# Element-wise work of w_up's operands on Pool beside VectorE: one decoder layer on one core

## The chip, the cores and the metric

The kernel runs on one core of one Trainium2 chip. The metric is the device time of one execution in microseconds (us), lower is better. The engines of the core are TensorE (PE in the profile, its weight loads PEld), VectorE (DVE), ScalarE (ACT), Pool (POOL, also GpSimd) and SyncE (SP), which here only queues transfers (DMAs).

## What is computed

One layer of a decoder, for 512 tokens of a prompt and 8 samples of 8 new tokens, 576 tokens in all (NT = 576, HALF = 288), with a width of 2048 and a feed-forward width of 5632. A mixer (gated delta heads and mLSTM heads) comes first; then the part that this case is about, the convolutional feed-forward block:

```
h = _rmsnorm(x, norm_ffn_g)
u = jnp.einsum('bld,df->blf', h, w_up)
uc, ffn_new = _causal_dwconv(u, ffn_buf, ffn_conv_w)
uc = uc + ffn_conv_b.astype(f32)
gate, up = jnp.split(uc, 2, axis=-1)
x = x + jnp.einsum('blf,fd->bld', (jax.nn.silu(gate) * up).astype(x.dtype), w_down)
```

The width of `u` is 2 x 5632 = 88 tiles of 128 columns: 44 gate tiles and 44 up tiles. A final norm ends the layer.

## The kernel before, in words

**Numbers in two parts.** Each float32 operand of a large product is split (`split`, lines 118 to 121) into a high part, which ScalarE rounds (L120), and a low part, the difference, which VectorE computes (L121). Each product is then three: high by high, high by low and low by high. In the profile `wh` and `wl` are the parts of weights, `bh` and `bl` those of the right operands in the sevenfold form below, `ah` and `al` those of the activations in the plain form.

**Order.** TensorE's instructions stay in the order in which the program writes them. Those of the other engines are ordered by a scheduler when the program is built, by priorities and a cost model; `urgent` and `ahead` raise a priority. On the chip each engine then runs its own list strictly in that order, and each instruction waits for the semaphores it needs. Work that runs beside the products is written as generators: `spawn` adds one, and `tick` (called once for each 128 rows of a product) moves each of them one step on.

**The plain tiles of w_up.** The first three gate tiles and up tiles (NPL = 3) are plain products of 2048 rows (L198). The last of the three pairs is made by turns (`dense_pair`, line 220), so that the first rows of the activations are done with early. VectorE multiplies each result by the norm's factors into a buffer with pads for the convolution (L1130; the pads and the saved states are small Pool copies, L1074, L1075 and L1080). `conv_rest` (line 1078) convolves on ScalarE (L1083) and VectorE (L1085). `hidden` (line 1092) takes silu of the gate on ScalarE (L1094) and multiplies it by up on VectorE, 512 columns for the prompt (L1096) and 64 for the samples (L1097); `later` (line 183) then queues the store of the result on SyncE (L187), six ticks on.

**The seven products.** The other 41 pairs of tiles use seven products of half size in place of eight (`pair`, line 1274, products at L1265). They need sums and differences of the weights (VectorE, L1230) and, once for all pairs, of the normalised input: the right operands. `prep` (line 1164) makes these for each k of 0 to 7. It loads rows k and k + 8 of x (L1178, into `y`, two buffers for each of the two rows), multiplies them by the norm's factors (VectorE, L1179), and calls `right_operands` (line 1185), which forms four differences of 288 columns (L1188) in the tiles `y1`, `y2` and `t` (one buffer) and splits seven half-width operands in four steps, one of them half as wide. For k = 0 to 4 this runs as a generator beside the plain tiles. For k = 5 to 7 it runs in `seven_start` (line 1145), with a raised priority, as memory comes free: there the pools `b2` (their operands) and `ur` (weights) take over the memory of the plain form's activations.

The first pair's products 0, 4 and 5 are begun over k = 0 to 4 and then completed over k = 5 to 7 (in `pair`). The weights' loads (L129 plain, L1206 sevenfold), the loads of rows of x and the stores of hidden rows share SyncE's queue.

**Later.** w_down has blocks of plain and of seven products; `down_prep` (line 1414) calls the same `right_operands` for the latter. `pair` calls the same `hidden`.

Of the kernel before, what the change touches and what calls it, by code (L numbers as in the profile page):

```python
# [8 lines left out]
F32 = mybir.dt.float32  # L9
F32R = mybir.dt.float32r  # L10
AF = mybir.ActivationFunctionType
ALU = mybir.AluOpType

P = 128
D = 2048
KT = 16
SEQ = 512
NB = 8
# [9 lines left out]
KS = 6  # L28
# [15 lines left out]
# columns of the parameter array  # L44
G1, G2, G3, CW, DG, MG, FW, FBI, GB, AL, M0, NPAR = 0, 16, 32, 48, 144, 145, 153, 417, 505, 506, 507, 515
# columns of the constant array
C_ID, C_INC, C_LV, C_IS, C_BM, C_SG, C_BD, C_RB, C_M3, NCON = 0, 128, 256, 640, 704, 712, 713, 841, 849, 853

# order of the 128-column tiles of w_in
# [19 lines left out]
class Layer:  # L69
# [25 lines left out]
    def open(self, name, **k):  # L95
        """A pool that close() ends (last in, first out on its side of the memory)."""
        stack = ExitStack()
        self.stacks[name] = stack
        return stack.enter_context(self.tc.tile_pool(name=name, **k))
# [57 lines left out]
    def down_weights(self, b):  # L157
        """The weights of the plain blocks from b on, up to the next one of seven products."""
        while b < len(BLOCKS) and BLOCKS[b][1] == FB:
            for mp in range(8):  # L160
                yield self.I["w_down"][sum(n == FB for _, n in BLOCKS[:b]), mp], b == len(BLOCKS) - 1
            b += 1

# [19 lines left out]
    def later(self, n, out, in_):  # L183
        """A store, queued n steps from now."""
        def gen():
            yield n
            self.nc.sync.dma_start(out=out, in_=in_)  # L187
        self.spawn(gen(), prio=False)
# [12 lines left out]
    def dense(self, outs=None):  # L201
        """One 128-column tile of a K=2048 product."""
        pd = None
        if outs is None:
            pd = self.psd()
            outs = (pd[:, 0, 0:HALF], pd[:, 1, 0:HALF])
        for u in range(2):
            for i, part in enumerate(self.unit()):
                self.dense_part(outs, part, 2 * u + i)
        return pd  # L210
# [9 lines left out]
    def dense_pair(self):  # L220
        """Two tiles by turns, so that the first rows of the input are done with early."""
        pds = [self.psd(), self.psd()]
        for u in range(2):
            for pd in pds:
                for i, part in enumerate(self.unit()):
                    self.dense_part((pd[:, 0, 0:HALF], pd[:, 1, 0:HALF]), part, 2 * u + i)
        return pds
# [22 lines left out]
    def sum_bc(self, ss):  # L250
        """Sums over partitions of ss [P, NT], on all partitions."""
        pss = []
        for hf in range(2):
            pr = self.psr()
            sl = slice(hf * HALF, (hf + 1) * HALF)
            self.nc.tensor.matmul(pr[:, 0:HALF], self.ones, ss[:, sl], start=True, stop=True)  # L256
            pss.append((pr[:, 0:HALF], sl))
        return pss
# [139 lines left out]
    def gate_rows(self, outs):  # L398
# [19 lines left out]
        # softplus(y) = max(y, 0) + log1p(exp(-|y|)), log1p(e) = 2 atanh(e / (2 + e))  # L418
# [40 lines left out]
        # gated delta rows: log decay G, -exp(G), exp(Glast - G)  # L459
# [6 lines left out]
        # mLSTM rows (partitions 64-67)  # L466
# [51 lines left out]
    def conv_in(self, t, pd):  # L518
        """Depthwise convolution and silu of a projected tile."""
# [27 lines left out]
    def decay(self, bc, cols):  # L547
        """exp(min(bc_i - col_j, 0)) on and above the diagonal, else 0 (rows j, columns i)."""
        nc = self.nc
        V, A, Pl = nc.vector, nc.scalar, nc.gpsimd  # L550
        em = self.r()
        for c in range(NCH):
            sl = slice(c * CH, c * CH + CH)
            V.tensor_scalar(out=em[:, sl], in0=bc[:, sl], scalar1=cols[c][0], scalar2=0.0, op0=cols[c][1], op1=ALU.min)
        V.tensor_scalar(out=em[0:64, SEQ:NT], in0=bc[0:64, SEQ:NT], scalar1=cols[4][0], scalar2=0.0, op0=cols[4][1], op1=ALU.min)
        A.activation(em[:, 0:SEQ], em[:, 0:SEQ], AF.Exp)
        A.activation(em[0:64, SEQ:NT], em[0:64, SEQ:NT], AF.Exp)
        ev = em[:, 0:SEQ].rearrange("p (c i) -> p c i", c=NCH)
        Pl.tensor_tensor(out=ev, in0=ev, in1=self.bc4(self.con[:, C_INC:C_INC + P]), op=ALU.mult)
        Pl.tensor_tensor(out=em[0:64, SEQ:NT], in0=em[0:64, SEQ:NT], in1=self.con[0:64, C_IS:C_IS + 64], op=ALU.mult)  # L560
        return em
# [7 lines left out]
    def lasts_of(self, bc):  # L569
        """The columns of bc at each chunk's last token."""  # L570
        t = self.sm(12, "last")
        A = self.nc.scalar
        A.copy(t[:, 0:4], bc[:, 0:SEQ].rearrange("p (c i) -> p c i", c=NCH)[:, :, CH - 1])
        A.copy(t[:, 4:12], bc[:, SEQ:NT].rearrange("p (b i) -> p b i", b=NB)[:, :, LS - 1])
        return t

    def dn_head(self, h, q, k, v, sz):
# [14 lines left out]
        # natural k, norms of k  # L592
# [30 lines left out]
        # U = c_j (k_j . k_i) E, KQ = (k_j . q_i) E  # L623
# [19 lines left out]
        # v / |k| natural  # L643
# [18 lines left out]
        # chunk by chunk over the prompt  # L662
# [32 lines left out]
        # output norm; the scale of q only enters through the guard  # L695
# [10 lines left out]
    def pack(self, t, n, tag, order):  # L706
        """32 rows of t at a time as three groups of rows, each the high or the low parts."""
# [11 lines left out]
    def masked_rows(self, vp, g, b, nb):  # L719
        """The rows of vp for nb samples from b on, side by side, with zeros for the other samples' tokens."""  # L720
# [46 lines left out]
    def inverse(self, U, res, more):  # L767
        """X = (I + U)^-1 for the strictly upper part of U: the diagonal blocks of SB by substitution, block by
        block on the partitions, then by doubling."""
# [58 lines left out]
        # blocks of 32 from those of 16  # L828
# [19 lines left out]
        # blocks of 64 from those of 32  # L848
# [19 lines left out]
        # the whole blocks  # L868
# [200 lines left out]
    def conv_pads(self, f):  # L1069
        """A buffer for the depthwise convolution: [2 zeros, prompt, 8 x (2 old, 8 new tokens)]."""  # L1070
        rb = self.rw()
        pads = rb[:, 514:594].rearrange("p (b w) -> p b w", b=NB)
        with self.urgent():
            self.nc.gpsimd.memset(rb[:, 0:2], 0.0)  # L1074
            self.nc.gpsimd.tensor_copy(pads[:, :, 0:2], f[:, 1:9])  # L1075
        return rb, (rb[:, 2:2 + HALF], rb[:, 2 + HALF:514], pads[:, :, 2:10])
# [11 lines left out]
    def psum_parts(self, p0, p1):  # L1088
        """The three parts of conv_pads' buffer in two products by halves of the tokens."""
        return (p0, p1[:, 0:SEQ - HALF], p1[:, SEQ - HALF:HALF].rearrange("p (b w) -> p b w", b=NB))  # L1090

    def hidden(self, j, g, u, o):
# [3 lines left out]
        nc.vector.tensor_tensor(out=o[:, 0:SEQ], in0=g[:, 0:SEQ], in1=u[:, 0:SEQ], op=ALU.mult)  # L1096
        nc.vector.tensor_tensor(out=o[:, SEQ:NT].rearrange("p (b w) -> p b w", b=NB), in0=sv(g), in1=sv(u), op=ALU.mult)  # L1097
        self.later(6, self.hid[j], o[:, 0:NT])

    def ffn(self):  # L1100
# [6 lines left out]
        for j in range(NPL):  # L1107
# [24 lines left out]
            self.hidden(j, hs[0][0], hs[1][0], hs[0][1])  # L1132
# [12 lines left out]
    def seven_start(self):  # L1145
        """After the last plain products: the other right operands and the first left ones."""
# [17 lines left out]
    def prep(self, k0, k1, pool):  # L1164
        """The right operands of the seven half-size products, in two parts, of the rows k and k + 8 of the
        normalised input B: [B11, T3, B21, B22, T1, T2, T4]."""
# [7 lines left out]
        for k in range(k0, k1):  # L1174
# [7 lines left out]
            self.right_operands(*both[k - k0], *y, self.stg.tile([P, NT], F32, tag="t", name=self.nm("t")))  # L1182
            yield YP

    def right_operands(self, hi, lo, y1, y2, t):
        V = self.nc.vector
        A0, A1 = slice(0, HALF), slice(HALF, NT)
        sub = lambda o, a, b: V.tensor_tensor(out=o, in0=a, in1=b, op=ALU.subtract)  # L1188
# [11 lines left out]
    def operands(self):  # L1200
        """The left operands of the seven products of each pair of tiles of w_up, in the order of their use."""
# [72 lines left out]
    def pair(self, j, fst, steps):  # L1274
        """A gate tile and its up tile by seven products of half the size (Winograd's form of Strassen's)."""
# [52 lines left out]
        self.hidden(j, g, u, rg)  # L1328
# [85 lines left out]
    def down_prep(self, f0):  # L1414
        """The right operands of the seven products for the hidden rows f0 + k and f0 + KS + k."""
        self.bh, self.bl = [], []
        both = [[self.sx.tile([P, 7 * HALF], F32R, tag=f"b{n}{k}", name=self.nm("b" + n)) for n in "hl"] for k in range(KS)]
        for k in range(KS):
            y1, y2 = (self.load_hidden(self.r(), f0 + k + KS * i) for i in range(2))
            self.right_operands(*both[k], y1, y2, self.r())  # L1420
            yield

    def down_operands(self, ns):
        """The left operands of the seven products of each pair of tiles of w_down, in the order of their use."""
# [52 lines left out]
    def down_last(self, acts):  # L1477
        """The last block by tokens, so that the final norm of one part runs beside the other part's products."""
# [163 lines left out]
```

## Time and profile before

| | us |
|---|---|
| three runs, median (lowest to highest) | 2703.66 (2702.69 to 2705.25) |
| span of the profiled execution | 2704.9 |
| busy: TensorE / VectorE / ScalarE / Pool | 2661.1 / 1992.4 / 1072.4 / 327.8 |
| the last plain product of w_up ends | 1236.15 |

The page gives the span of the profiled execution, from its first instruction to its last; no other time is listed for that execution. It lies inside the three runs.

How to read the views: a row of the list of waits names the engine that waited, its tile and line, what it waited for, and then the total, the number of waits and the longest, in us. A row of the timeline gives start, length, engine, line, operation, output and inputs with their shapes, a count if several were merged, and in brackets the idle time before it with its releaser. A row for one line gives the shortest, median and longest duration in ns, then the first and the last start in us. `x1024` is a number of columns for each of 128 partitions. Successive VectorE instructions overlap by a little in these records.

### The profile page before, as it was taken

How to read it: one execution, taken by the hardware profiler on the slowest of the kernel's cores; microseconds unless marked ns; L12 is line 12 of the kernel's file. 1: busy time of each engine (PE TensorE's matmuls, PEld its weight loads, DVE VectorE, ACT ScalarE, POOL GpSimd, SP SyncE). 2: the span in 40 equal slices, each digit the busy share in tenths (PEclk: the TensorE clock that was granted, in tenths of full speed). 3: DMA queues.
4: the chain of work that ended last, by engine and by line, in shares of the span. 5: the costliest groups of instructions: out<-in, count | busy, mean ns of one | idle time of the engine just before them, and what ended most of it. 6: DMA issues, size and time to landing. Idle time of an engine off the chain costs nothing.

```text
span 2704.9 us, 48701 instructions
## 1 busy us (share of the span) xinstructions
PE 2661.1 (98%) x19895; PEld 2620.4 (97%) x19895; DVE 1992.4 (74%) x3346; ACT 1072.4 (40%) x1694; POOL 327.8 (12%) x637
## 2 busy tenths in 40 slices
PE   7999999999999999998999999999999999999998
PEld 7999999999999999998999999999999999999998
DVE  7887777764444332289888888888888888988656
ACT  5334344433333232254444444444444443434324
POOL 2223222222111001111000000000000100000001
PEclk9999999999999999999999999999999999999999
DMA  5222222223332334444333333333333373342333
GB/s 195 85 79 92 91 83 91 91 88 105 112 107 89 122 127 134 137 124 149 107 107 107 109 111 110 107 107 107 107 107 107 107 255 99 105 145 71 121 96 100
DMA packets 112233, 304.02 MB, mean 112 GB/s; under 512 B 21912, under 2 KB 28184, under 8 KB 112008
## 3 DMA queue, kind: packets, MB, share of 16 engines
q1 hardware_dynamic: 107896, 291.17, 34.1%
q0 software_dynamic: 1872, 7.37, 0.8%
q8 instruction: 156, 2.56, 0.4%
q10 hardware_dynamic: 2240, 2.36, 0.3%
q14 instruction: 69, 0.57, 0.1%
HBM read 264.79 MB, written 36.06 MB: 111 GB/s over the span
## 4 chain that ended last, share of the span: by engine, by line
PE 88%; DVE 4%; DMA 1%; ACT 1%; issue 1%; POOL 0%; SPq 0%; DVEq 0%
PE pd L198 35%; PE pr L1265 31%; PE pd L1265 12%; PE pr L198 3%; PE pr L1491 1%; DMA r<-hid 1%; PE pr L991 1%; DVE wl L121 1%; PE pr L737 1%; DVE bl L121 0%; POOL irk L613 0%; DVE r L1526 0%; PE pr L832 0%; PE pr L256 0%; ACT r L603 0%
## 5 line engine op out<-in xcount | busy, mean ns | idle before, releaser
L120 ACT CAST wh<-raw 128x1024 fp32r<-128x1024 f32 (+1 forms) x394 | 404.6, 1027 | 744.7 <-PE pd L198 410.6
L1265 PE MATMUL pr<-bh,wh 128*128 128x288 f32 x2120 | 627.5, 296 | 2.2 <-ACT bh L120 2.2
L1265 PE MATMUL pr<-bl,wh 128*128 128x288 f32 x2120 | 625.0, 295 | 0.7 <-DVE bl L121 0.6
L1265 PE MATMUL pr<-bh,wl 128*128 128x288 f32 x2120 | 625.2, 295 | 0.1
L121 DVE TENSOR_TENSOR wl<-raw,wh 128x1024 fp32r<-128x1024 f32 (+1 forms) x394 | 474.4, 1204 | 183.3 <-ACT wh L120 177.0
L198 PE MATMUL pd<-ah,wh 128*128 128x288 f32 x2496 | 558.4, 305 | 0.0
L198 PE MATMUL pd<-ah,wl 128*128 128x288 f32 x2496 | 534.4, 296 | 0.0
L198 PE MATMUL pd<-al,wh 128*128 128x288 f32 x2496 | 534.2, 296 | 0.0
L198 PEld LDWEIGHTS pd<-ah,wh 128*128 128x128 f32 x2496 | 401.0, 189 | 9.5 <-issue 2.9
L198 PEld LDWEIGHTS pd<-ah,wl 128*128 128x128 f32 x2496 | 401.9, 189 | 0.0
L1265 PEld LDWEIGHTS pr<-bl,wh 128*128 128x128 f32 x2120 | 400.7, 189 | 1.1 <-DVE bl L121 1.1
L198 PEld LDWEIGHTS pd<-al,wh 128*128 128x128 f32 x2496 | 401.8, 189 | 0.0
L1265 PEld LDWEIGHTS pr<-bh,wh 128*128 128x128 f32 x2120 | 399.3, 188 | 2.4 <-ACT bh L120 2.4
L1265 PEld LDWEIGHTS pr<-bh,wl 128*128 128x128 f32 x2120 | 399.5, 188 | 0.8 <-DVE wl L121 0.8
L120 ACT CAST wh<-s 128x1024 fp32r<-128x1024 f32 (+1 forms) x171 | 169.5, 991 | 362.9 <-DVE s L1230 139.3
L1265 PE MATMUL pd<-bh,wh 128*128 128x288 f32 x848 | 252.0, 297 | 5.6 <-ACT wh L120 5.6
L1265 PE MATMUL pd<-bh,wl 128*128 128x288 f32 x848 | 250.9, 296 | 1.7 <-DVE wl L121 1.7
L1265 PE MATMUL pd<-bl,wh 128*128 128x288 f32 x848 | 249.9, 295 | 0.0
L121 DVE TENSOR_TENSOR wl<-s,wh 128x1024 fp32r<-128x1024 f32 (+1 forms) x171 | 196.5, 1149 | 27.0 <-ACT wh L120 19.6
L1265 PEld LDWEIGHTS pd<-bh,wh 128*128 128x128 f32 x848 | 160.2, 189 | 6.1 <-ACT wh L120 6.1
L1265 PEld LDWEIGHTS pd<-bh,wl 128*128 128x128 f32 x848 | 160.7, 189 | 2.3 <-DVE wl L121 2.3
L1265 PEld LDWEIGHTS pd<-bl,wh 128*128 128x128 f32 x848 | 160.9, 190 | 0.0
(391 smaller groups left out, 3514.1 us busy)
## 6 DMA issues: line engine op xcount, KB each, us to landing
raw<-in_w_up SPq DMA_DIRECT2D x176, 512.0 KB
raw<-in_w_in SPq DMA_DIRECT2D x114, 512.0 KB
raw<-in_w_down SPq DMA_DIRECT2D x40, 512.0 KB
raw<-in_w_out SPq DMA_DIRECT2D x32, 512.0 KB
raw<-in_w_down SPq DMA_DIRECT2D x40, 384.0 KB
hid<-r SPq DMA_DIRECT2D x44, 288.0 KB
r<-hid SPq DMA_DIRECT2D x40, 288.0 KB
r<-in_xT SPq DMA_DIRECT2D x32, 288.0 KB
```

The lines of the kernel that those rows point to most:

```text
L120: nc.scalar.copy(hi, src)
L121: nc.vector.tensor_tensor(out=lo, in0=src, in1=hi.bitcast(F32), op=ALU.subtract)
L198: mm(outs[hf], w, x[:, hf * HALF:(hf + 1) * HALF], start=first and i == 0, stop=last and i == 2)
L737: mm(pr[:, 16 * b:16 * b + 16], st[:, b], kqs[:, b].rearrange("p a w -> p (a w)"), start=True, stop=True)
L991: mm(pn[0:64, 0:257], self.qim[:, b], caug[b // 4][:, b % 4], start=b == 0, stop=False)
L1265: mm(out, w[:, ks], x[:, sl], start=k == 0 and i == 0, stop=k == nk - 1 and i == 2)
L1491: mm(pr[:, 0:n], w[:, ks], acts[kk][:, a * NT + sl.start:a * NT + sl.stop], start=kk == 0 and i == 0, stop=kk == FB - 1 and i == 2)
```

## The change

`hidden` and `right_operands` get the engine as a parameter. The three plain pairs of tiles pass Pool to `hidden`, `pair` passes VectorE as before. `prep` passes Pool to `right_operands`, `down_prep` passes VectorE as before. The splits' differences (L121) stay on VectorE, and so does the multiplication by the norm's factors (L1179). Nothing else differs but comments, which keep their lines as empty ones.

```
-    def hidden(self, j, g, u, o):
+    def hidden(self, j, g, u, o, e):
...
-        nc.vector.tensor_tensor(out=o[:, 0:SEQ], in0=g[:, 0:SEQ], in1=u[:, 0:SEQ], op=ALU.mult)
-        nc.vector.tensor_tensor(out=o[:, SEQ:NT].rearrange("p (b w) -> p b w", b=NB), in0=sv(g), in1=sv(u), op=ALU.mult)
+        e.tensor_tensor(out=o[:, 0:SEQ], in0=g[:, 0:SEQ], in1=u[:, 0:SEQ], op=ALU.mult)
+        e.tensor_tensor(out=o[:, SEQ:NT].rearrange("p (b w) -> p b w", b=NB), in0=sv(g), in1=sv(u), op=ALU.mult)
...
-            self.hidden(j, hs[0][0], hs[1][0], hs[0][1])
+            self.hidden(j, hs[0][0], hs[1][0], hs[0][1], Pl)
...
-            self.right_operands(*both[k - k0], *y, self.stg.tile([P, NT], F32, tag="t", name=self.nm("t")))
+            self.right_operands(*both[k - k0], *y, self.stg.tile([P, NT], F32, tag="t", name=self.nm("t")), nc.gpsimd)
...
-    def right_operands(self, hi, lo, y1, y2, t):
-        V = self.nc.vector
+    def right_operands(self, hi, lo, y1, y2, t, e):
...
-        sub = lambda o, a, b: V.tensor_tensor(out=o, in0=a, in1=b, op=ALU.subtract)
+        sub = lambda o, a, b: e.tensor_tensor(out=o, in0=a, in1=b, op=ALU.subtract)
...
-        self.hidden(j, g, u, rg)
+        self.hidden(j, g, u, rg, V)
...
-            self.right_operands(*both[k], y1, y2, self.r())
+            self.right_operands(*both[k], y1, y2, self.r(), self.nc.vector)
```

## The prediction

> **What bounds the kernel now.** I read the page's busy shares first, then the list of what TensorE waited for, then the stretches around the place that the change touches, and last each engine's order of time there.
>
> ```profile
> PE 2661.1 (98%) x19895; PEld 2620.4 (97%) x19895; DVE 1992.4 (74%) x3346; ACT 1072.4 (40%) x1694; POOL 327.8 (12%) x637
> ...
> PE pd L1265 <- ACT wh L120: 4.0, 1, 4.0
> PE pr L1265 <- ACT bh L120: 2.2, 1, 2.2
> PE pd L1265 <- DVE wl L121: 0.9, 1, 0.9
> PE pr L1265 <- DVE bl L121: 0.6, 1, 0.6
> ```
>
> TensorE (PE) is busy for 98% of the span, so work taken off VectorE (DVE) can only pay where TensorE waits for it. The four lower rows are all the waits of TensorE between 1130 and 1300 us, the stretch that holds every moved instruction: 7.7 us in all. The stretches place them (columns: length, then busy time of PE, PEld, DVE, ACT, POOL, granted clock, DMA):
>
> ```profile
> 1172.00:1229.00 57.00, 57.00 (x429) 57.00 (x428) 54.68 (x95) 27.53 (x39) 5.25 (x12) 1.00 0.47 144
> 1229.00:1236.15 7.15, 7.15 (x56) 7.15 (x55) 4.07 (x7) 4.58 (x7) 1.87 (x3) 1.00 0.04 15
> ...
> 1236.15:1242.15 6.00, 1.97 (x16) 1.74 (x15) 5.61 (x9) 1.44 (x3) 0.00 (x0) 0.91 0.75 234
> 1242.15:1247.23 5.08, 4.13 (x16) 3.79 (x16) 5.08 (x10) 2.08 (x4) 0.54 (x2) 0.50 0.69 252
> ...
> 1250.65:1254.10 3.45, 0.66 (x3) 0.45 (x4) 3.45 (x6) 1.50 (x3) 0.00 (x0) 1.00 0.37 122
> 1254.10:1258.05 3.95, 3.95 (x21) 3.95 (x20) 3.95 (x6) 2.73 (x5) 0.72 (x1) 0.58 0.12 35
> ```
>
> Until 1236.15 the last plain tiles of w_up run and TensorE never stops, although VectorE is nearly full. Then the seven products begin, and TensorE stands twice: 1238 to 1244 and 1250.65 to 1254. After each stand its granted clock is about half for some 4 us (0.50, 0.58). In both VectorE is full. This handover is the one place where the change can move the end.
>
> **The change, part by part.** It moves 32 subtractions of 128x288 (four for each of eight row pairs k) and three pairs of products (128x512 and 128x64) from VectorE to Pool.
>
> ```profile
> L1188 DVE TENSOR_TENSOR t<-y x8: 447/450/456, 1181.9 to 1250.1; 128x288 f32<-128x288 f32 x8
> L1499 POOL TENSOR_TENSOR r<-r,r x12: 732/868/1223, 2649.4 to 2690.5; 128x320 f32<-128x320 f32 x6, 128x256 f32<-128x256 f32 x6
> 1147.91 1.77 POOL L1052 TENSOR_TENSOR r<-r,r 128x576 f32<-128x576 f32 x1 [11.78 <-ACT r L1051]
> L1038 DVE SCALAR_TENSOR_TENSOR al<-r,par,ah x16: 805/805/1830, 1147.6 to 1163.6; 128x576 fp32r<-128x576 f32 x16
> ```
>
> One subtraction takes VectorE 0.45 us, of which 0.08 overlaps its successor (two that follow each other start 0.37 apart, below): 0.37 us come free for each. On Pool the nearest row is L1499: 0.73 us for its 256 columns at the least, 0.87 in the middle, mostly 320; for 288 I take 0.80.
>
> These 0.80 us do not run wholly beside VectorE. The last row shows VectorE's slowest case, 1830 ns in place of 805, and it is the one during which Pool's 576-column addition runs: VectorE was held for 1.03 us. Half the columns hold it for half, 0.53 us (estimate; it could be the whole 0.80). So each moved subtraction frees 0.37 and holds 0.53: VectorE loses 0.16 us a piece where it is full, and its own instruction in progress first delays Pool's. The Trainium skill ("SBUF — State Buffer", Who interferes with whom) says that a VectorE instruction with two SBUF inputs and a Pool one that reads SBUF exclude each other, whichever starts first; the trace agrees with its 1830 ns.
>
> *Plain tiles, to 1236 us: 0.* Twenty subtractions of k = 0 to 4 and three of k = 5 cost VectorE 23 x 0.16 = 3.7 us; the products of tiles 0 and 1 at 512 columns hold 0.94 and free some 0.6, twice, 0.7 more. Against 4.4 us stand idle 57.00 - 54.68 + 7.15 - 4.07 = 5.4 us. The cover is thin, but the operands are first read after 1236, and the weights' splits that TensorE reads here come ahead of need: TensorE waits for none. Without the cover the excess would land on the handover, a few tenths of a us.
>
> ```profile
> L1096 DVE TENSOR_TENSOR r<-r,r x44: 682/691/693, 1196.4 to 2173.5; 128x512 f32<-128x512 f32 x44
> L814 POOL TENSOR_TENSOR r<-r,con x16: 1277/1494/2012, 124.0 to 600.0; 128x512 f32<-128x512 f32 x16
> 1197.20 0.32 SPq L187 DMA_DIRECT2D hid<-r  x1
> 1199.88 0.33 SPq L129 DMA_DIRECT2D raw<-in_w_up  x1
> 1272.59 0.33 SPq L187 DMA_DIRECT2D hid<-r  x1
> 1276.87 3.10 SPq L1206 DMA_DIRECT2D raw<-in_w_up  x2
> ```
>
> *silu(gate) * up: 0.* The product grows from 0.69 to about 1.49 us (0.8 later), the small one, an eighth of the columns, by 0.1 (estimate), and each may wait a VectorE instruction. Its store stands in SyncE's queue ahead of weight loads; those went out 2.7 us (first tile) and 4.3 us (third) after the store, so 1 to 3 us more are covered, nearly. Pool's queue holds behind these only the small copies of the convolution's pads and states, needed a tile later, and the state's DMAs, for which TensorE does not wait.
>
> *Handover.* First VectorE, then ScalarE and SyncE, in order of time:
>
> ```profile
> 1236.17 0.76 DVE L1130 TENSOR_TENSOR r<-pd,rstd 128x288 f32<-128x288 f32 x2 [2.71 <-PE pd L198]
> 1236.85 0.75 DVE L121 TENSOR_TENSOR bl<-y,bh 128x576 fp32r<-128x576 f32 x1
> ...
> 1238.18 1.42 DVE L121 TENSOR_TENSOR bl<-y,bh 128x576 fp32r<-128x576 f32 x2
> 1239.71 1.22 DVE L1230 TENSOR_TENSOR s<-raw,raw 128x1024 f32<-128x1024 f32 x1
> 1240.86 0.45 DVE L1188 TENSOR_TENSOR y<-y,t 128x288 f32<-128x288 f32 x1
> 1241.57 0.82 DVE L1179 SCALAR_TENSOR_TENSOR y<-y,par,rstd 128x576 f32<-128x576 f32 x1 [0.26 <-DMA y<-x2d]
> ...
> 1242.67 1.22 DVE L121 TENSOR_TENSOR wl<-s,wh 128x1024 fp32r<-128x1024 f32 x1
> 1243.81 0.45 DVE L121 TENSOR_TENSOR bl<-y,bh 128x288 fp32r<-128x288 f32 x1
> 1244.17 1.22 DVE L1230 TENSOR_TENSOR s<-s,raw 128x1024 f32<-128x1024 f32 x1
> ...
> 1246.55 1.22 DVE L121 TENSOR_TENSOR wl<-s,wh 128x1024 fp32r<-128x1024 f32 x1
> ...
> 1249.40 0.80 DVE L1179 SCALAR_TENSOR_TENSOR y<-y,par,rstd 128x576 f32<-128x576 f32 x1
> ...
> 1251.63 0.45 DVE L1188 TENSOR_TENSOR y<-y,y 128x288 f32<-128x288 f32 x1
> 1252.00 0.45 DVE L1188 TENSOR_TENSOR t<-y,t 128x288 f32<-128x288 f32 x1
> ```
> ```profile
> 1234.11 0.66 ACT L120 CAST bh<-y 128x576 fp32r<-128x576 f32 x1
> 1236.17 0.33 SPq L1206 DMA_DIRECT2D raw<-in_w_up  x1
> 1237.62 0.33 SPq L1178 DMA_DIRECT2D y<-x2d  x1
> ...
> 1244.29 0.33 SPq L1178 DMA_DIRECT2D y<-x2d  x1
> ```
> ```profile
> 1237.62 3.92 DMA y<-x2d
> ```
>
> The stall of 4.0 us ends with the first sum s of weights (1239.71) and its cast. The sum needs the weights asked for at 1236.17, as the last plain product freed their memory, and a smaller load asked for at 1237.62 took 3.92 us; so VectorE cannot bring the sum much forward: 0, or up to 0.53 later behind one Pool hold.
>
> The stall of 0.9 us ends with the split wl at 1242.67, which the same VectorE queue delivers after a subtraction, the norm and another subtraction. The next sum and split follow (1244.17, 1246.55), just in time for TensorE at 1247.2. I take the freed subtractions here as used up by Pool's holds, and two holds more in this chain: +1.1 us (ends: -0.9, the stall gone, and +2.1, four holds).
>
> The two last stalls, 2.2 + 0.6 us, wait for k = 7. Its second row could be loaded only at 1244.29, when k = 5's last split (1243.81) had let go of the buffer; that split needed the subtraction at 1240.86, which queued on VectorE behind splits and the sum, though its input was split by 1238.9. On Pool it starts then: waiting 0.7 for VectorE's split, 0.8, a cast of 0.4 and a split of 0.4 bring the load to about 1241.9, landing 3.92 later at 1245.8. Norm (0.8, after a wait of 1), a Pool subtraction (0.8 and 0.7 of waiting), cast and split (0.7 each) end near 1250.5, and TensorE, itself 1.1 later, asks for them near 1251.5. So 2.8 us go: -2.8. What is late next is the sum of weights, counted above.
>
> With that stand its slow clock goes too: 3.95 x (1 - 0.58) = 1.7 us. The Trainium skill ("TensorE: Matmul & The Clock Gate", What's actually happening) has the clock fall after an idle window of about 3.4 us; by that, stalls of 2.2 and 0.6 us need not have cost it and I would forecast 1.7 us less gain. The row says 0.58, and the measurement decides.
>
> Sum: 0 + 0 + 1.1 - 2.8 - 1.7 = -3.4 us. The profiled span is 2704.9 us, 1.2 above the median of 2703.66 and inside the three runs (2702.69 to 2705.25); taken off the median it is **2700.3 us**.
>
> **Rivals.** Measurement can tell some 0.2% here, 5.4 us.
>
> *Pool's chain becomes the late one (slower).* Each subtraction of k = 7 on which its casts wait would take 0.80 plus a wait for a VectorE split of up to 1.14, in place of 0.37: three make 4.7 us, and four holds in the weights' chain 2.1 us, while stalls and slow clock stay: +6.8, 2710.5 us. It decides once k = 7's subtractions end after about 1252. For: the 1830 ns, and VectorE full. Against: in the old order these stood behind weights' sums anyway. Chance 0.15.
>
> *No earlier than before.* Each engine's order is fixed when the program is made. If the norm of k = 7's second row keeps its place (1249.40), the subtraction ends at 1250.1 + 0.8 + up to 1.1 = 1252.0, where it ends now: 2703.7 us, give or take 1. Chance 0.18.
>
> *All but the first stall goes.* VectorE sat 2.71 us before 1236.17, its queue standing at L1130, while the cast of 1234.11 had made its next split ready. With fewer instructions the order may put those splits first; then no hold falls into the weights' chain: -2.8 - 0.9 - 1.7 = -5.4, and 1 or 2 more if the clock of 0.50 recovers sooner: 2696.5 to 2698.3 us. Chance 0.25.
>
> **How the numbers follow.** The forecast has 0.42 (its own range 2698.5 to 2703). Faster by over 5.4 us: 0.15 of the third rival and 0.02 of the forecast. Slower: 0.12 of the first. The rest, 0.71, is within 0.2%. The range 2696 to 2709.5 leaves out the ends of the third and the first, some 0.15.
>
> **What would show it.** Right: TensorE waits for bh or bl after 1250 are gone, the stretch after has clock 1.00, the second y load goes out before 1243, subtractions on Pool take 0.8 to 1.9 us, and some VectorE instructions there are 0.5 longer. The forecast is wrong if TensorE waits in the plain tiles, if the sum at 1239.7 starts over 1 us later, or if TensorE's waits change after 1270, where I expect none.

## The result, and the profile after

The change makes the kernel slower by about 17 us, three times the 5.4 us that the prediction held for measurable.

| | before | after |
|---|---|---|
| median of 4 runs each (lowest to highest), us | 2704.1 (2702.69 to 2705.25) | 2722.34 (2719.01 to 2724.08) |
| ratio, 95% interval | | 1.0063 [1.0051, 1.0076] |
| span of the profiled execution, us | 2704.9 | 2722.3 |
| last plain product of w_up ends, us | 1236.15 | 1250.42 |

Of the 17.4 us between the spans, 14.3 lie ahead of the last plain product (1250.42 - 1236.15) and 3.1 behind it. The forecast had put nothing at all into the first part.

Lines of the changed kernel stand one lower behind line 1186: the subtractions are L1187, the weights' sums L1229, the loads L1205, the seven products L1264. First its busy shares:

```profile
PE 2666.9 (98%) x19895; PEld 2624.7 (96%) x19895; DVE 1991.6 (73%) x3308; ACT 1073.2 (39%) x1694; POOL 373.8 (14%) x675
```

The work did move: VectorE has 38 instructions fewer and Pool 38 more, 46.0 us of them. But VectorE's busy time fell by 0.8 us only; what stayed on it grew by nearly as much as was taken off. Then what TensorE waited for from 1130 to 1300 us (total, times, longest):

```profile
PE pd L1264 <- ACT wh L120: 7.4, 1, 7.4
PE pd L198 <- DVE r L1130: 3.6, 1, 3.6
PE pd L198 <- ACT wh L120: 2.8, 2, 2.1
PE pd L198 <- DVE wl L121: 2.3, 3, 1.2
PE pr L1264 <- DVE wl L121: 1.3, 2, 1.0
PE pd L1264 <- DVE wl L121: 0.6, 1, 0.6
PE pr L1264 <- ACT wh L120: 0.6, 1, 0.6
PE pr L1264 <- DVE bl L121: 0.4, 1, 0.4
```

The three L198 rows are new: 8.7 us of waiting inside the plain tiles, where there was none. The first stall of the sevenfold products is 7.4 us in place of 4.0. The wait for bh (2.2 us before) is gone. The stretches show the rest of the loss (length, then PE, PEld, DVE, ACT, POOL, granted clock, DMA):

```profile
1172.00:1229.00 57.00, 48.28 (x340) 46.82 (x339) 51.87 (x64) 25.79 (x37) 34.34 (x37) 0.95 0.40 122
1229.00:1250.50 21.50, 21.50 (x146) 21.50 (x145) 7.65 (x10) 6.97 (x10) 4.32 (x5) 0.88 0.20 64
```

TensorE stands for 8.7 us of the first stretch, and its clock is below 1 in both; the 14.3 us are 8.7 of standing and, by difference, 5.6, nearly all of it running slowly (0.05 of 48.28 us and 0.12 of 21.50 us make 5.0). VectorE, though, is *less* busy than before (51.87 of 57 us; it was 54.68). It is not out of time; it waits. For what, the timeline shows: first ScalarE ahead of TensorE's wait at 1215.78, then TensorE's rows with its three longest waits:

```profile
1214.35 0.43 ACT L120 CAST bh<-y 128x288 fp32r<-128x288 f32 x1 [2.97 <-POOL y L1187]
1214.69 1.04 ACT L120 CAST wh<-raw 128x1024 fp32r<-128x1024 f32 x1
```
```profile
1215.78 0.54 PE L198 MATMUL pd<-ah,wh 128*128 128x288 f32 x2 [2.13 <-ACT wh L120]
1217.46 0.85 PE L198 MATMUL pd<-ah,wl 128*128 128x288 f32 x2 [0.87 <-DVE wl L121]
1228.53 0.82 PE L198 MATMUL pd<-ah,wh 128*128 128x288 f32 x2 [3.63 <-DVE r L1130]
```

ScalarE's list holds the cast of a right operand (bh), which waits 2.97 us for Pool, *ahead of* the cast of a weight (wh) for which TensorE stands. TensorE reads no bh before 1250. Not all of this is Pool's own work. Its subtraction took 1.23 us, and ahead of it Pool had stood 2.38 us for VectorE, whose split still read the buffer that the subtraction writes:

```profile
1213.09 1.23 POOL L1187 TENSOR_TENSOR y<-y,t 128x288 f32<-128x288 f32 x1 [2.38 <-DVE bl L121]
```

The longest of the three waits, 3.63 us, is not ScalarE's. TensorE stands for an evacuation: L1130, with which VectorE reads a finished result and so frees its buffer. VectorE takes the first part of that result at 1222.91 us and the rest at 1227.87, behind a split of weights and three norms, two of them beside Pool's subtractions (together 2.61 us; two took 1.54 to 1.56 before):

```profile
1225.34 2.61 DVE L1179 SCALAR_TENSOR_TENSOR y<-y,par,rstd 128x576 f32<-128x576 f32 x2
1227.87 0.51 DVE L1130 TENSOR_TENSOR r<-pd,rstd 128x224 f32<-128x224 f32 x2
```

In the kernel before, only a split of 1.22 us stands between the parts of the same result (1211.17 to 1212.97 us). So VectorE's list had changed too.

ScalarE's order of 1214 us stands at the handover again, in ScalarE's timeline and then in VectorE's row for the sum:

```profile
1254.65 0.43 ACT L120 CAST bh<-y 128x288 fp32r<-128x288 f32 x1 [3.92 <-POOL y L1187]
1257.34 0.67 ACT L120 CAST bh<-y 128x576 fp32r<-128x576 f32 x1 [2.26 <-POOL y L1187]
1258.10 0.67 ACT L120 CAST bh<-t 128x576 fp32r<-128x576 f32 x1
1258.67 1.04 ACT L120 CAST wh<-s 128x1024 fp32r<-128x1024 f32 x1
```
```profile
1254.02 1.67 DVE L1229 TENSOR_TENSOR s<-raw,raw 128x1024 f32<-128x1024 f32 x1
```

The sum s is done at 1255.69; its cast starts 3.0 us later, behind two casts of k = 6, the first of which waits for Pool. In the kernel before, it started 0.1 us behind the sum (which ended at 1239.71 + 1.22 = 1240.93), ahead of a cast of k = 5 and of all those of k = 6, as ScalarE's timeline of before shows:

```profile
1241.05 1.05 ACT L120 CAST wh<-s 128x1024 fp32r<-128x1024 f32 x1 [4.56 <-DVE s L1230]
1242.00 0.43 ACT L120 CAST bh<-y 128x288 fp32r<-128x288 f32 x1
```

The last view of the changed kernel is that of its moved line on Pool (shortest, median, longest in ns) and of who waited for it:

```profile
L1187 POOL TENSOR_TENSOR t<-y x8: 861/1312/3029, 1179.6 to 1263.6; 128x288 f32<-128x288 f32 x8
L1187 POOL TENSOR_TENSOR y<-y,y x8: 802/897/1666, 1181.1 to 1266.7; 128x288 f32<-128x288 f32 x8
L1187 POOL TENSOR_TENSOR t<-y,t x8: 791/1308/1790, 1182.8 to 1267.5; 128x288 f32<-128x288 f32 x8
L1187 POOL TENSOR_TENSOR y<-y,t x8: 807/1236/1316, 1186.4 to 1268.4; 128x288 f32<-128x288 f32 x8
...
  ACT bh L120: 53.6, 34
```

The shortest subtraction takes 0.79 us, three of the four kinds 1.2 to 1.3 in the median, and ScalarE stood 53.6 us in all behind them.

### The profile page after: what moved, and what is told of

It reads as the page before. It is cut to its first block, busy times and chain, and to the rows that moved or that the text cites. A ratio compares the mean times of both kernels' runs of the same rounds, so it can differ in the third digit from the quotient of the medians.

```text
span 2722.3 us, 48713 instructions
## 1 busy us (share of the span) xinstructions
PE 2666.9 (98%) x19895; PEld 2624.7 (96%) x19895; DVE 1991.6 (73%) x3308; ACT 1073.2 (39%) x1694; POOL 373.8 (14%) x675
## 4 chain that ended last, share of the span: by engine, by line
PE 86%; DVE 5%; issue 1%; POOL 1%; ACT 1%; DMA 1%; DVEq 0%; POOLq 0%; ACTq 0%
PE pd L198 33%; PE pr L1264 31%; PE pd L1264 12%; PE pr L198 3%; PE pr L1490 1%; DVE bl L121 1%; DVE wl L121 1%; PE pr L991 1%; PE pr L737 0%; POOL y L1187 0%; POOL irk L613 0%; DVE r L1525 0%; DMA r<-hid 0%; POOL t L1187 0%; PE pr L832 0%
## 5 line engine op out<-in xcount | busy, mean ns | idle before, releaser
L1264 PE MATMUL pr<-bh,wh 128*128 128x288 f32 x2120 | 627.6, 296 | 0.8 <-ACT wh L120 0.6
L1264 PE MATMUL pr<-bh,wl 128*128 128x288 f32 x2120 | 625.3, 295 | 1.3 <-DVE wl L121 1.3
L1264 PE MATMUL pr<-bl,wh 128*128 128x288 f32 x2120 | 624.9, 295 | 0.4 <-DVE bl L121 0.4
L121 DVE TENSOR_TENSOR wl<-raw,wh 128x1024 fp32r<-128x1024 f32 (+1 forms) x394 | 476.4, 1209 | 189.0 <-ACT wh L120 182.7
L198 PE MATMUL pd<-ah,wh 128*128 128x288 f32 x2496 | 560.2, 306 | 6.4 <-DVE r L1130 3.6
L198 PE MATMUL pd<-ah,wl 128*128 128x288 f32 x2496 | 536.3, 297 | 2.3 <-DVE wl L121 2.3
L198 PE MATMUL pd<-al,wh 128*128 128x288 f32 x2496 | 535.5, 296 | 0.0
L198 PEld LDWEIGHTS pd<-ah,wh 128*128 128x128 f32 x2496 | 402.5, 190 | 16.7 <-issue 6.8
L198 PEld LDWEIGHTS pd<-ah,wl 128*128 128x128 f32 x2496 | 403.1, 189 | 3.0 <-DVE wl L121 3.0
L198 PEld LDWEIGHTS pd<-al,wh 128*128 128x128 f32 x2496 | 403.0, 189 | 0.0
L1264 PEld LDWEIGHTS pr<-bl,wh 128*128 128x128 f32 x2120 | 400.7, 189 | 0.8 <-DVE bl L121 0.8
L1264 PEld LDWEIGHTS pr<-bh,wl 128*128 128x128 f32 x2120 | 399.6, 188 | 2.0 <-DVE wl L121 2.0
L1264 PEld LDWEIGHTS pr<-bh,wh 128*128 128x128 f32 x2120 | 399.3, 188 | 1.2 <-ACT wh L120 0.9
L1264 PE MATMUL pd<-bh,wh 128*128 128x288 f32 x848 | 252.0, 297 | 9.0 <-ACT wh L120 9.0
L1264 PE MATMUL pd<-bh,wl 128*128 128x288 f32 x848 | 250.8, 296 | 1.4 <-DVE wl L121 1.4
L1264 PE MATMUL pd<-bl,wh 128*128 128x288 f32 x848 | 249.8, 295 | 0.0
L121 DVE TENSOR_TENSOR wl<-s,wh 128x1024 fp32r<-128x1024 f32 (+1 forms) x171 | 196.8, 1151 | 26.0 <-ACT wh L120 18.5
L1264 PEld LDWEIGHTS pd<-bh,wh 128*128 128x128 f32 x848 | 160.2, 189 | 9.4 <-ACT wh L120 9.4
L1264 PEld LDWEIGHTS pd<-bh,wl 128*128 128x128 f32 x848 | 160.6, 189 | 2.0 <-DVE wl L121 2.0
L1264 PEld LDWEIGHTS pd<-bl,wh 128*128 128x128 f32 x848 | 160.9, 190 | 0.1
```

The costliest lines, as they stand in the source:

```text
L121: nc.vector.tensor_tensor(out=lo, in0=src, in1=hi.bitcast(F32), op=ALU.subtract)
L198: mm(outs[hf], w, x[:, hf * HALF:(hf + 1) * HALF], start=first and i == 0, stop=last and i == 2)
L1264: mm(out, w[:, ks], x[:, sl], start=k == 0 and i == 0, stop=k == nk - 1 and i == 2)
```

## The experiments

Three theories stood at the start. **A, order:** the lists of ScalarE and VectorE put work that waits for Pool ahead of work that TensorE needs. **B, held VectorE:** while Pool reads SBUF, VectorE's instructions with two operands in SBUF stand, and VectorE falls behind. **C, stores:** the later silu(gate) * up holds back the weight loads in SyncE's queue. Each run has its own runs of the kernel before beside it. A ratio of 1.0010 is 2.7 us.

| run | median, us | before, us | ratio, 95% interval |
|---|---|---|---|
| e1_hidden_only | 2706.31 | 2705.43 | 1.0003 [0.9994, 1.0013] |
| e2_early_only | 2717.02 | 2705.43 | 1.0043 [1.0028, 1.0057] |
| e3_late_only | 2707.26 | 2705.43 | 1.0007 [0.9998, 1.0017] |
| e4_pool_beside | 2711.61 | 2705.43 | 1.0022 [1.0013, 1.0032] |
| e5_early_behind | 2709.70 | 2705.13 | 1.0014 [1.0005, 1.0022] |
| e6_late_behind | 2708.36 | 2705.13 | 1.0014 [1.0005, 1.0023] |
| e7_before_behind | 2705.54 | 2705.13 | 1.0000 [0.9991, 1.0009] |
| e8_full_behind | 2712.63 | 2705.13 | 1.0027 [1.0016, 1.0037] |
| e9_pool_writes | 2705.54 | 2705.48 | 1.0001 [0.9992, 1.0010] |
| e10_one | 2705.66 | 2705.48 | 1.0001 [0.9992, 1.0010] |
| e11_one_behind | 2705.20 | 2705.48 | 1.0002 [0.9992, 1.0011] |
| e12_before_both | 2708.13 | 2705.24 | 1.0009 [1.0000, 1.0018] |

### The three parts alone

e1_hidden_only moves only the plain tiles' products; `prep` passes VectorE as before.

> Only the two products of silu(gate) and up of the three plain tiles run on Pool; all differences stay on VectorE. Theory A (queue): in the changed kernel ScalarE's in-order queue holds the cast of the next weights behind casts of right operands that wait for Pool's subtractions; so this part alone costs nothing, 0 to +1 us against before. Theory B (port): Pool's reads hold VectorE, which is late with splits and evacuations; six instructions hold some 3 us, 0 to +1 us. Theory C (store): the hidden rows' stores, later now, stand in SyncE's queue ahead of weight loads; then this part alone brings most of the loss, +8 us or more.

e2_early_only moves only the subtractions of k = 0 to 4, e3_late_only only those of k = 5 to 7:

```
-            self.right_operands(*both[k - k0], *y, self.stg.tile([P, NT], ...))
+            self.right_operands(*both[k - k0], *y, self.stg.tile([P, NT], ...), nc.gpsimd if k < KB1 else V)   # e2
+            self.right_operands(*both[k - k0], *y, self.stg.tile([P, NT], ...), V if k < KB1 else nc.gpsimd)   # e3
```

> Only the differences of k = 0 to 4 (beside the plain tiles) run on Pool. A (queue): TensorE stands in the plain tiles as in the changed kernel, +10 to +14 us against before, with its waits released by ScalarE's wh cast or by splits right behind it. B (port): +8 to +14 us, with VectorE full all through that stage. C (store): under +4 us.

> Only the differences of k = 5 to 7 (the handover) run on Pool. A (queue): no wait in the plain tiles; at the handover the cast of the first sum of weights stands behind casts of k = 6 that wait for Pool, the first stall grows from 4.0 to about 7 us, the last ones shrink: +2 to +4 us against before. B (port): +1 to +3 us, from VectorE's sums and splits starting later by Pool's holds. The forecast on record for this part: -3.4 us.

The products alone cost nothing that can be measured (+0.9 us), so C falls. The early subtractions alone cost 11.6 us, the late ones 1.8, within what the measurement leaves open. Together the three make 14.3 of the 17 to 18 us; the rest is their meeting, or the spread of the medians. e2_early_only has the order of the changed kernel again, three casts that wait for Pool ahead of a weight's (ScalarE's timeline), and a stall of 3.2 us behind it (TensorE's):

```profile
1209.69 0.68 ACT L120 CAST bh<-y 128x576 fp32r<-128x576 f32 x1 [1.44 <-POOL y L1187]
1210.99 0.67 ACT L120 CAST bh<-t 128x576 fp32r<-128x576 f32 x1 [0.62 <-POOL t L1187]
1212.25 0.43 ACT L120 CAST bh<-y 128x288 fp32r<-128x288 f32 x1 [0.59 <-POOL y L1187]
1212.59 0.69 ACT L1094 ACTIVATE r<-r 128x592 f32<-128x592 f32 x1
1213.19 1.03 ACT L120 CAST wh<-raw 128x1024 fp32r<-128x1024 f32 x1
```
```profile
1214.27 0.53 PE L198 MATMUL pd<-ah,wh 128*128 128x288 f32 x2 [3.20 <-ACT wh L120]
1216.05 0.77 PE L198 MATMUL pd<-ah,wl 128*128 128x288 f32 x2 [0.98 <-DVE wl L121]
1226.12 0.58 PE L198 MATMUL pd<-ah,wh 128*128 128x288 f32 x2 [2.42 <-DVE r L1130]
```

e3_late_only is what the forecast's step on the late stalls speaks of, and shows both of its sides. All waits of TensorE from 1130 to 1300 us in e3_late_only:

```profile
PE pd L1264 <- ACT wh L120: 7.3, 1, 7.3
PE pr L1264 <- DVE wl L121: 1.0, 1, 1.0
PE pd L1264 <- DVE wl L121: 0.7, 1, 0.7
PE pr L1264 <- ACT wh L120: 0.6, 1, 0.6
PE pr L1264 <- DVE bl L121: 0.2, 1, 0.2
```

The second load of y goes out at 1242.10 us, and of the two late waits (2.2 and 0.6 us) 0.2 are left. But the first wait has grown from 4.0 to 7.3, and the gain is gone.

### Pool's work without its place in any list

e4_pool_beside keeps every subtraction on VectorE. It adds four subtractions a k on Pool, for k = 0 to 4, that read the finished right operand and write a scratch tile which nobody reads. e9_pool_writes adds in their place one copy of a column and twelve fills a k; the fills write SBUF and read nothing. Both do more work than the kernel before, none of it used.

```
             if k < KB1:
                 hi, z = both[k - k0][0].bitcast(F32), self.stg.tile([P, HALF], F32, tag="z", name=self.nm("z"))
e4:              for i in range(4):
                     nc.gpsimd.tensor_tensor(out=z, in0=hi[:, i * HALF:(i + 1) * HALF], in1=hi[:, (i + 1) * HALF:(i + 2) * HALF], op=ALU.subtract)
e9:              nc.gpsimd.tensor_copy(z[:, 0:1], hi[:, 7 * HALF - 1:7 * HALF])
                 for i in range(12):
                     nc.gpsimd.memset(z, 0.0)
```

> All differences stay on VectorE; for each of k = 0 to 4 Pool makes four more subtractions of 128x288 that read finished right operands and write a scratch tile that nobody reads. So Pool's reads are there, but nothing waits for them. A (queue): -1 to +2 us against before. B (port): most of the loss of the differences' move comes without the move, +6 us or more, since VectorE now holds its own subtractions as well.

> All differences stay on VectorE, and silu(gate) * up too. For each of k = 0 to 4 Pool does added work that nobody uses: one copy of a single column of the finished right operand (so that it starts at the time of e4_pool_beside's subtractions) and then 12 fills with zeros of a 128x288 scratch tile, about 0.33 us each, some 4 us of Pool time for each k, as much as the four added subtractions of e4_pool_beside would take undisturbed (4 x 0.80 = 3.2) or a little less than they took (4 x 1.30 = 5.2). The fills write SBUF and read nothing. Theory B (what costs is that Pool's reads of SBUF hold VectorE's instructions): 0 to +1 us against before, where e4_pool_beside lost 6.2 (its run against before, 2711.61 - 2705.43); VectorE's instructions beside the fills keep their own durations (a subtraction 0.45 us, a split wl 1.22, a norm 0.81), and TensorE has no wait before 1236 us. Rival B' (any instruction of Pool, or the work queued on it, costs this much): +3 to +7 us, VectorE's instructions longer beside the fills, and a TensorE wait in the plain tiles as in e4_pool_beside (3.1 us).

Nobody waits for Pool in either. Yet e4_pool_beside loses 6.2 us, and e9_pool_writes, with more Pool time in the same stretch, nothing. First e4_pool_beside, then e9_pool_writes, over the stretch of the plain tiles:

```profile
1172.00:1229.00 57.00, 53.88 (x385) 53.62 (x385) 56.15 (x84) 25.28 (x35) 29.40 (x28) 0.94 0.36 116
```
```profile
1172.00:1229.00 57.00, 57.00 (x430) 57.00 (x429) 54.38 (x96) 27.00 (x39) 33.53 (x77) 1.00 0.46 146
```

With the fills Pool is busy for 33.53 us (20.4 of them are fills), VectorE stays at 54.38 us and TensorE at 57.00. With the reading subtractions Pool is busy for 29.40 us, and VectorE is busy to 56.15 while it finishes fewer instructions (84 for 95 before). Single ones show the hold, in the timeline of VectorE and then of Pool in e4_pool_beside (there four subtractions that follow each other, to 1214.76):

```profile
1213.02 1.06 DVE L1192 TENSOR_TENSOR t<-y 128x288 f32<-128x288 f32 x1
1214.01 1.37 DVE L1179 SCALAR_TENSOR_TENSOR y<-y,par,rstd 128x576 f32<-128x576 f32 x1
```
```profile
1208.28 6.48 POOL L1186 TENSOR_TENSOR z<-bh 128x288 f32<-128x288 f32 x4
```

The two take 0.45 and 0.81 us when Pool does not read: one Pool subtraction of 288 columns holds VectorE for 0.56 to 0.61 us. Twenty of them at 0.56, if each holds once, are 11.2 us, against the 5.4 us that VectorE had idle there; the 5.8 us of difference are nearly the loss of 6.2, though that is a sum of sizes and no trace of each. The loss comes out as one stall of 3.1 us, for the evacuation L1130 in VectorE's queue, and the slow clock after it. The Trainium skill ("SBUF — State Buffer", Who interferes with whom) says that a VectorE instruction with two SBUF inputs contends with a Pool instruction that reads SBUF and not with one that only writes it. The two runs agree: 6.2 us lost against 0.1.

### The order put right

In e5_early_behind to e8_full_behind the subtractions run on Pool, but ScalarE's list is tied: `issue_after` sets the casts of the right operands behind a given cast in ScalarE's order. For k = 0 to 4 that is the last loaded weight's cast, for k = 6 the cast of the weights' first sum and for k = 7 that of the second. For k = 6 and 7 the weights' sums are also written one a step (`SEVEN = (1, 1, 1)` for `(1, 0, 2)`).

```
+            with self.tc.issue_after(self.wcast.ins) if k < KB1 else ExitStack():      # e5
+            with self.tc.issue_after(self.opcast.ins) if k > KB1 else ExitStack():     # e6, e7
                 self.right_operands(...)
```

e5_early_behind is e2_early_only with this order, e6_late_behind is e3_late_only with it, e7_before_behind has e6_late_behind's order with all work on VectorE, and e8_full_behind is the whole change with both orders.

> As the run with only k = 0 to 4 on Pool (+11.6 us), same Pool instructions, but the casts of these right operands are queued on ScalarE behind the cast of the weights loaded last, so that no weights' cast stands behind one that waits for Pool. Theory A (queue order): TensorE's waits for wh and wl in the plain tiles (5.2 us of stand, and most of the slow clock behind it) go; 0 to +5 us against before, what is left being an evacuation held up. Theory B (port): Pool reads as much beside the same VectorE work, so +9 us or more stay.

> As the run with only k = 5 to 7 on Pool (+1.8 us, first stall 7.3 us), but the first sum of weights is written ahead of k = 6, and the casts of k = 6 and 7 are queued behind the weights' casts. A (queue order): the first stall returns to about 4.2 us while the late ones stay short: -4 to -1 us against before. B (port): VectorE's sum and splits are held as much as without the edit, +1 to +3 us.

> Control for the run before it in this list: the same order of k = 6 and 7 behind the weights' casts, with all differences on VectorE. -1 to +1.5 us against before by A and by B; if this gains as much as its pair on Pool, the gain is the order's and not Pool's.

> The whole change (differences and the plain tiles' products on Pool) with both orders of queues of the two runs before. A (queue order): -3 to +4 us against before, in place of +18. B (port): +12 us or more.

The order gives back about 7 of e2_early_only's 11.6 us (4.6 are left), and 10 of the whole change's 17 to 18 (7.5 are left). In e5_early_behind the plain tiles have 0.7 us of waits in place of 7.6, and the wait for L1130 is gone as well: the tie changed VectorE's order too, so the step from the one run to the other is not ScalarE's alone. Nor does the tie clear ScalarE's list in the way that its expectation says: at 1217.98 us of e5_early_behind a cast still waits 3.66 us for Pool, right ahead of a weight's cast. TensorE did not stand for that one: the weights' casts now come early enough.

In e8_full_behind all that TensorE waits for in the plain tiles is

```profile
PE pd L198 <- DVE wl L121: 1.1, 2, 0.8
```

and the last plain product ends at 1237.70 us, 1.5 later than before. What it still loses comes after that, at the handover: its waits there are 13.0 us (the first 6.3), for 7.7 before, in the slowest of its eight executions (2715.16 us).

For the late subtractions the order gives nothing back in total (1.0014 for 1.0007), though the first wait is 4.2 us again as theory A has it. What takes its place is B, beside its control e7_before_behind. First the two longest of TensorE's waits in e6_late_behind, then the timeline of VectorE and of Pool before the second of them:

```profile
PE pd L1265 <- ACT wh L120: 4.2, 1, 4.2
PE pd L1265 <- DVE wl L121: 3.3, 1, 3.3
```
```profile
1242.38 1.84 DVE L1230 TENSOR_TENSOR raw<-raw,raw 128x1024 f32<-128x1024 f32 x1
1244.14 1.81 DVE L121 TENSOR_TENSOR wl<-s,wh 128x1024 fp32r<-128x1024 f32 x1
```
```profile
1242.24 0.89 POOL L1188 TENSOR_TENSOR y<-y,y 128x288 f32<-128x288 f32 x1
1243.08 1.79 POOL L1188 TENSOR_TENSOR t<-y,t 128x288 f32<-128x288 f32 x1
```

A sum and a split of weights take 1.84 and 1.81 us in place of 1.22, just where TensorE stands for the split: 3.3 us, where the control waits 0.8.

### One subtraction alone

If a hold costs 0.6 us and an earlier load of y is worth some us, one subtraction on Pool should pay. e10_one moves only the last one of k = 5, on which that load depends; e11_one_behind does so in e7_before_behind's order.

```
         last, e = e, self.nc.vector          # e is Pool for k = 5, VectorE else
...
         e = last
         sub(y2[:, A0], y2[:, A0], t[:, A1])
```

> One subtraction alone goes to Pool: the last one of k = 5, on which the release of the buffer for the second y load of k = 7 depends; everything else stays on VectorE. The forecast's step on the late stalls: the second y load goes out near 1242 us instead of 1244.3, the two late waits (2.2 + 0.6 us) are gone and their slow clock with them, -2.8 - 1.7 = -4.5 us; with less than the whole of it, -1 to -3. Theory A (order in ScalarE's queue by the plan's times): as e3_late_only, where the load came at 1242.1, the late waits went but the first wait grew from 4.0 to 7.3 us because casts that wait for Pool stood ahead of the weights' casts; with one such cast only, the growth is smaller, 0 to 1 us, or appears if the order turns: between -3 and +1. Theory B: one subtraction on Pool holds VectorE once, 0.55 us, which the first wait can show at most once: 0 to +0.6 beside whatever the late waits give.

> As e10_one, and the casts of k = 6 and 7 are queued on ScalarE behind the casts of the weights' first sums, as in e6_late_behind and e7_before_behind (the same order of the seven products as there, one operand of each kind a step). e7_before_behind, with that order and all on VectorE, stands level with before (1.0000). Forecast's step: -1 to -4.5 us against before. Theory A: the first wait keeps its 4.0 to 4.2 us, since no cast that waits for Pool can stand ahead of a weights' cast. Theory B: one hold of 0.55 us, against e6_late_behind's several (+2.8 us over e7_before_behind): 0 to +0.6 us over e7, so level with before unless the earlier y load pays.

Neither differs from before. In e10_one the load goes out at 1241.74 us, 2.6 earlier, and the wait for bh falls from 2.2 to 1.0 us, no further: VectorE comes to k = 7's subtractions (1250.35 to 1251.67) only when its queue does, as the rival "No earlier than before" had it. The other waits grow by as much; all of them together are 7.6 us, for 7.7. One of them grows by the hold, which VectorE's sum shows in the timeline of e10_one:

```profile
1239.71 1.63 DVE L1231 TENSOR_TENSOR s<-raw,raw 128x1024 f32<-128x1024 f32 x1
```

That sum took 1.22 us before, and the first wait is 4.4 us for 4.0.

### The orders without Pool

e12_before_both is the control for e8_full_behind: both orders, all work on VectorE.

> The control for e8_full_behind: its two orders on ScalarE (casts of k = 0 to 4 behind the last loaded weights' cast, casts of k = 6 and 7 behind the casts of the weights' first sums), with every subtraction and product on VectorE, so no Pool work at all. Theory B (what e8_full_behind still loses, 7.5 us, is Pool holding VectorE): level with before, -1 to +1 us, no TensorE wait in the plain tiles, the first stall of the handover near 4.0 us. Rival A' (the orders themselves cost that, whichever engine subtracts, because a right operand's cast now waits for a weights' cast): +3 to +7 us, with the first stall near e8_full_behind's 6.3 us and the wait for bh near its 3.4 us.

It is 2.4 us slower than before, at the edge of what can be measured [0.0, 4.9], with a first wait of 4.7 us and a wait for bh of 2.8. (These waits are from the quickest of its eleven executions, 2704.45 us, and may be longer in the others.) That lies between what the two theories expected: the orders may cost something themselves. Of e8_full_behind's 7.5 us some 4.5 to 5 are then left for Pool's holds (2712.63 - 2708.13 = 4.5; ratios 1.0027 and 1.0009), with intervals of 2 to 3 us each way on both. e5_early_behind has no such control, so how its 4.6 us divide stays open. So does why the scheduler's list gives those casts so early a place: its order was seen and undone, the prices by which it chose were not.

No version here beats the kernel before.

## Why the prediction was wrong, step by step

- **What bounds the kernel: right.** TensorE is busy for 98% in both, and nearly all that was lost is time in which it stands or runs at the slow clock that follows.
- **Plain tiles, "0": the step that failed.** It cost 14.3 us. The step set the net loss of VectorE (4.4 us) against VectorE's idle time (5.4 us) and said that "the weights' splits that TensorE reads here come ahead of need". The price of a hold was about right: 0.41 to 0.62 us in the rows shown here, where the step had 0.53. That of a subtraction on Pool was not: mostly 1.2 to 1.3 us beside VectorE, where the step had 0.80. What the step left out is that each engine runs one list in order. It had asked who reads the right operands (TensorE, not before 1236 us), not what is queued behind their casts on ScalarE. There stood the weights' casts, and as each subtraction took longer and also passed from VectorE to Pool and on to ScalarE, the casts kept ScalarE standing: 5.1 of the 8.7 us of waits are for weights. The other 3.6 are VectorE's list, where an evacuation stood behind norms; e4_pool_beside has such a stall (3.1 us) from holds alone, with the evacuation in its old place, so how these 3.6 divide stays open. Tying the order removed nearly all of it: in e8_full_behind TensorE waits 1.1 us in the plain tiles, for 8.7.
- **silu(gate) * up, "0": right.** e1_hidden_only, 1.0003 [0.9994, 1.0013], though a 512-column product takes 2.2 us on Pool here (the median of three), not 1.49.
- **Handover, first stall, "0, or up to 0.53 later": failed.** It grew by 3.4 us. The hold is in it, as written (the sum took 1.67 us for 1.22, 0.45 more); the other 2.9 are the sum's cast behind k = 6's casts. The forecast followed the sum on VectorE and did not look at ScalarE's list behind it. e6_late_behind, with the list tied, has 4.2 us.
- **Weights' chain, "+1.1" (up to +2.1): in its range in the changed kernel, too small behind a short first stall.** In the changed kernel the waits for weights behind the first stall are 2.5 us for 0.9 before, 1.6 more, but a stall of 7.4 us stands ahead of them. In e6_late_behind, where that one is 4.2, the split's wait is 3.3 us against 0.8 in its control: 2.5 more.
- **Second load of y at "about 1241.9": right** (1242.10 in e3_late_only, 1241.74 in e10_one), in part by luck. Its terms as written (1238.9 and 0.7, 0.8, 0.4, 0.4) add up to 1241.2; in e10_one Pool took 1.24 us for 0.7 + 0.8, and the last split then came only at 1241.26, behind the longer sum. **"-2.8" and "-1.7" for it: right in place, worth nothing in sum.** e3_late_only loses those late waits and 3.3 us elsewhere; in e10_one, where nothing else is moved, 1.7 of their 2.8 us are still there.
- **The rivals.** "Pool's chain becomes the late one" had the sign and a chance of 0.15, but another place: it spoke of k = 7's subtractions after 1252 us, and the casts that did the harm belong to k = 2, 3 and 6, whose results TensorE was not waiting for. Its 6.8 us were short of 17. "All but the first stall goes" (0.25) had the sign the other way, and it was the first stall that grew. The forecast's own test, "TensorE waits in the plain tiles", is the one that came out against it.

In short, of some 17 us the tied order takes away about 10 (17.0 less the 7.3 of e8_full_behind, by ratios). Of those 7.3 the control with the orders alone has 2.4, which is the tie's own cost and not in the changed kernel, and about 5 are left for Pool's holds. If the parts add up, which no run shows, order is worth 10 to 12 of the 17 us and the holds about 5.

## What to carry to other kernels

When a step moves to a slower engine, follow not only its reader but every instruction queued *behind* that reader on the reader's engine: a result that nobody needs yet can still stop the machine through a list that is run in order. Idle time of an engine, added up over a stretch, is no cover for such a wait. And Pool is no free second VectorE for work with both operands in SBUF: count what each of its reads takes from VectorE, and compare that with what the move frees.

## What was not expected of the hardware

- A Pool subtraction of 128x288 takes 0.79 us by itself and mostly 1.2 to 1.3 beside a full VectorE, once 3.03: VectorE holds Pool as well. In e11_one_behind, with VectorE standing, it took 0.79; in e10_one, beside the sum above, 1.24.
- Pool's writes cost VectorE nothing: 60 fills of 128x288, 20.4 us of them, and the norm's multiplication L1179 kept 807 to 821 ns (804 to 820 before; up to 1369 in e4_pool_beside).
- In these runs a stall of 3 to 4 us cost about half as much again. After the waits of 3.63 us (changed kernel) and 3.12 us (e4_pool_beside) the granted clock was 0.50 for the next 3.8 us, as the rows of the stretches right behind them show, first the changed kernel's, then e4_pool_beside's:

```profile
1228.53:1232.37 3.84, 3.84 (x16) 3.84 (x17) 2.81 (x3) 1.70 (x2) 1.54 (x4) 0.50 0.00 0
```
```profile
1220.13:1224.00 3.87, 3.87 (x16) 3.87 (x17) 3.87 (x6) 2.03 (x3) 2.62 (x5) 0.50 0.40 139
```

- That is 3.84 x 0.5 = 1.9 us on top of 3.63. The Trainium skill ("TensorE: Matmul & The Clock Gate", What's actually happening) has the clock fall after an idle window of about 3.4 us. Here 3.12 us were enough, and in e2_early_only 2.42 us were followed by a clock of 0.56 for 3.9 us.
